# Accumulating row transfers, the gate's first weights behind the last experts, and statistics tied to the neighbouring tile, in a one-core decoder layer

## The chip, the cores and the metric

The kernel runs on one core of a Trainium2 chip. Its engines are TensorE (PE, with PEld for its weight loads), VectorE (DVE), ScalarE (ACT), GpSimd (POOL) and SyncE (SP, which here only issues transfers); 16 DMA engines move data. The metric is the device time of one execution in microseconds, as the median of several runs.

## The reference, cut to what matters

One layer over 512 tokens of 2048 numbers, all float32:

```python
y = concat([s5(u), conv(v, g)]) @ w_o + b_o
h = layer_norm(alpha * x + y, ln1)
m = hierarchical_moe(h)            # 32 experts, 2 per token; hidden width 256
h = layer_norm(alpha * h + m, ln2)
e = (p @ w_p) * sigmoid(h @ w_pg + b_pg)
x = layer_norm(alpha * h + e, ln3)
```

In the mixer every token's two experts compute `silu(t @ w_gate) * (t @ w_up)`, weighted, times `w_down`; `m` is the sum of the two results.

## The kernel before, in words

Tokens are 4 tiles of 128 (`NT`), features 16 chunks of 128 (`KD`). The first part (input projection, state space group, convolution group, output projection, first layer norm, routing) ends at about 675 us and is not touched. `p @ w_p` is made there too and kept in DRAM (`p_dram`), but for the last token tile's, which comes later at line 1210; until then the two `raw` buffers hold `w_p`.

**Experts (lines 1077 to 1282).** The 32 experts are packed in 14 groups (`GROUPS`) of 128 token slots; a group holds 1, 2 or 4 experts. For each group `gather` fetches its 128 token rows from `h_dram` into `gx` (an indirect transfer from POOL's queue), `columns` transposes them into `xt`, `up` multiplies by the gate and up weights in four quarters, `act` makes the activations `at`, `down` multiplies by the down weights in two halves, and `scatter` writes the result rows to `y_dram` (two indirect transfers, one for each half of the columns; two rows for each token, one for each of its experts). All weights come once, in 192 loads of 1 MiB from SP's queue (`ring_load`) into a ring of buffers: 15 of its own at first, and after group 1 the two `raw` buffers, which line 1213 puts at the head of the ring. A load waits until the products on its buffer's former contents are done, and SP issues in order. Loads of the first group and two quarters of the second are called for ahead (`early`, `ahead1`).

In the round of group 0 stands a branch (line 1226) for experts with more tokens than their slots: all engines read a count `mo` and jump over its body where there is none, as with these inputs. The gather and transposes of group 1 follow it. `mo` lies in a column of `xt`.

**Tail (lines 1285 to 1437).** `tt[m]`, called `h2[m]` here, holds alpha times the first layer norm's result. `total(m)` loads the two y rows of each token of tile m (two transfers for each half of the columns), adds them, adds the sum to `h2[m]` and takes the statistics; `normalize(m)` makes the layer norm in four quarters, transposes each and splits it in two parts of reduced precision, `h2h` (ACT) and `h2l` (DVE). The product with `w_pg` goes in four column blocks c; each weight quarter of 1 MiB is split by `wsplit` in two halves of two parts (`whi` by ACT, `wlo` by DVE or POOL), and each product is three matmuls (`mm3`, lines 100 to 102). Block 0 goes tile by tile, right behind `normalize`; `gate` applies bias, sigmoid and `p`; block 3 ends with the last layer norm and the output.

The order on each engine's queue is set at build time by a planner that runs the program against a model of durations; engines then work through their queues in order, and a wait holds what is behind it. Pools release memory at `close()`, and a later tile in the same place waits for the former one's readers.

Of the kernel before, what the change touches and what calls it, by code (L numbers as in the profile page):

```python
# [8 lines left out]
FT = mybir.dt.float32  # L9
# [8 lines left out]
P = 128  # L18
# [36 lines left out]
def build(tc, I, out, dbg=None, stages=9):  # L55
# [1021 lines left out]
    s5 = top.enter_context(ExitStack())  # L1077
    if True:
        psE = s5.enter_context(tc.tile_pool(reuse_waits="tile", name="psE", bufs=1, space=PSUM))
        ep = s5.enter_context(tc.tile_pool(reuse_waits="tile", name="ep", bufs=1))  # L1080
# [4 lines left out]
        def big(name):  # L1085
            return ep.tile([P, D], FT, name=name)
# [11 lines left out]
        gx = big("gx")  # L1098
        ring += [big(f"ring{n}") for n in (13, 14)]
        ring = [ring[0], *ring[4:], last, ring[1], ring[2], ring[3]]  # L1100
        turn = [0]

        def ring_load(src):
            t = ring.pop(0)
            ring.append(t)
            nc.sync.dma_start(t, src)
            return t
# [80 lines left out]
        ahead1 = [loads(1, 0)]  # L1188
        gather(sl1)
        V.tensor_copy(ids_, tab[:, 0:NP])  # L1190
        columns()
        for i, (width, members) in enumerate(GROUPS):
            st = strips(width, members)
            gu = bank("gu", 2)
            if i + 1 < NGR and i:
                gather(sl0[:, i + 1:i + 2])
            for q in range(4):
                up(gu, st, early[q] if i == 0 else ahead1[q] if i == 1 and q < 2 else loads(i, q), q)
            at = act(gu, wt0[:, i:i + 1])
            if i + 1 < NGR and i:  # L1200
                columns()
            for q in range(2):
                down(at, st, early[4 + q] if i == 0 else loads(i, 4 + q), q, sl0[:, NGR + i:NGR + i + 1])
            if i == 1:

                for q in range(2):
                    for c in range(2):
                        ps = bank("dps", 4)
                        for k in range(2):
                            T.matmul(ps, pm[:, k], wps[q][:, k, c * 512:(c + 1) * 512], start=k == 0, stop=k == 1)  # L1210
                        (A.copy if c else V.tensor_copy)(pe_[:, c], ps)
                    G.dma_start(p_dram[NT - 1, 2 * q:2 * q + 2].rearrange("c p d -> p c d"), pe_)
                ring[:0] = [rpool.tile([P, D], FT, name="raw", tag="raw", bufs=2) for _ in range(2)]
            if i == 2:
# [7 lines left out]

            mo = xt[:, 0, 0:1].bitcast(I32)
            V.tensor_copy(mo, tab[:, 2 * NP:])
            most = nc.values_load(mo[0:1], min_val=0, max_val=S)
            with tc.If(most > 0):
# [28 lines left out]
                with tc.For_i(0, NP, 1) as n:  # L1255
                    mine = nc.values_load(tab[0:1, bass.ds(n + NP, 1)], min_val=0, max_val=S)
                    with tc.If(mine > 0):
                        e = bass.ds(nc.values_load(tab[0:1, bass.ds(n, 1)], min_val=0, max_val=NE - 1), 1)
                        for c in range(NOV):
                            with tc.If(mine > c * P):  # L1260
# [17 lines left out]
                                V.memset(gx, 0.0)  # L1278
            gather(sl0[:, 1:2])
            columns()  # L1280

# [3 lines left out]
    with ExitStack() as s5:  # L1285
# [20 lines left out]
        for n in range(2):  # L1306
            V.tensor_copy(pick[n], ident[0:8, 4 * n:4 * n + 4].unsqueeze(2).broadcast_to([8, 4, P]))

        raws = [rpool.tile([P, D], FT, name="raw", tag="raw", bufs=2) for _ in range(2)] + [fy.tile([P, D], FT, name=f"fr{n}") for n in range(2)]
        for q in range(3):  # L1310
            nc.sync.dma_start(raws[q], I["w_pg"][0, q])
        y0 = [fy.tile([P, 2, 1024], FT, name=f"y0{c}") for c in range(2)]
        hls = [wsplit(wF, raws[q], 8, (V, V) if q else (G, G)) for q in range(3)]
        for n in range(8):
# [4 lines left out]

        def load_y(r, m, c):  # L1320
            for q in range(2):
                nc.sync.dma_start(r[:, :, q * 512:(q + 1) * 512], yv[c][m, :, :, q * 512:(q + 1) * 512])

        for c in range(2):
            load_y(y0[c], 0, c)
        nc.sync.dma_start(raws[3], I["w_pg"][0, 3])
        hls.append(wsplit(wF, raws[3], 8, (G, G)))
        w_pg = ahead([lambda c=c, q=q: wsplit(wF, raw_load(I["w_pg"][c, q]), 8) for c in range(1, 4) for q in range(4)], 1)
# [26 lines left out]
        def total(m):  # L1355

            t = h2[m]
            st2 = fh.tile([P, 4, 6], FT, name="st2", bufs=2)
            if m:
                rs = [rpool.tile([P, 2, 1024], FT, name="raw", tag="raw", bufs=2) for _ in range(2)]  # L1360
                for c in range(2):
                    load_y(rs[c], m, c)
            else:
                rs = y0
            for c, r in enumerate(rs):
                for q in range(2):
                    i = slice(q * 512, (q + 1) * 512)
                    o = t[:, c * 1024 + q * 512:c * 1024 + (q + 1) * 512]
                    (G if m or q == 0 else V).tensor_tensor(r[:, 0, i], r[:, 0, i], r[:, 1, i], op=OP.add)
                    (G if m and not (m == 1 and q) else V).tensor_tensor(o, o, r[:, 0, i], op=OP.add)  # L1370
                    V.bn_stats(st2[:, 2 * c + q], o)
            return st2
# [18 lines left out]
        st2 = total(0)  # L1391
        fystk.close()
        fp = s5.enter_context(tc.tile_pool(reuse_waits="tile", name="fp", bufs=1))
        h2h = fp.tile([P, KD, S], FR, name="h2h")
# [108 lines left out]
```

## Time and profile before

| | us |
|---|---|
| Median of 3 runs | 1488.04 (1487.8 to 1489.32) |
| Profiled execution, its own time | 1486.21 |
| Its span, first to last instruction | 1484.5 |
| PE busy | 1264.4 (85%) |
| DVE busy | 784.1 (53%) |
| POOL busy | 392.9 (26%) |
| ACT busy | 376.4 (25%) |

Busy matmuls overlap one another, so a busy TensorE need not be at its peak; shares are means over stages with different limits, so a stage is read from its own window. The chain of waits is followed back from the last instruction to what released each step. A wait for several things is put down to the one that came last. SP's issues are not counted as busy; its waits have a view of their own. Where a line is a helper's (lines 79, 80, 100 to 102, 166 to 181), instructions are told apart by the tiles that they name.

### The profile page before, as it was taken

How to read it: one execution, taken by the hardware profiler on the slowest of the kernel's cores; microseconds unless marked ns; L12 is line 12 of the kernel's file. 1: busy time of each engine (PE TensorE's matmuls, PEld its weight loads, DVE VectorE, ACT ScalarE, POOL GpSimd, SP SyncE). 2: the span in 40 equal slices, each digit the busy share in tenths (PEclk: the TensorE clock that was granted, in tenths of full speed). 3: DMA queues.
4: the chain of work that ended last, by engine and by line, in shares of the span. 5: the costliest groups of instructions: out<-in, count | busy, mean ns of one | idle time of the engine just before them, and what ended most of it. 6: DMA issues, size and time to landing. Idle time of an engine off the chain costs nothing.

```text
span 1484.5 us, 16536 instructions
## 1 busy us (share of the span) xinstructions
PE 1264.4 (85%) x6128; PEld 805.0 (54%) x6129; DVE 784.1 (53%) x1275; ACT 376.4 (25%) x568; POOL 392.9 (26%) x327
## 2 busy tenths in 40 slices
PE   6999999989999999978488998787767774599996
PEld 4877878777777888843132322221111121388884
DVE  7999899789997643681011110010000006975567
ACT  4336555554333421121012100000000003023210
POOL 0368667864944200010010110000000005600000
PEclk9999999998999999989699999999889996699998
DMA  6344544536531362349659999999999995426413
GB/s 233 110 132 119 153 145 137 146 115 217 218 120 59 115 223 85 110 175 375 271 220 424 422 422 421 420 419 420 418 409 418 415 386 190 142 105 215 141 44 120
DMA packets 97448, 349.90 MB, mean 236 GB/s; under 512 B 29939, under 2 KB 43779, under 8 KB 61707
## 3 DMA queue, kind: packets, MB, share of 16 engines
q1 hardware_dynamic: 51152, 303.21, 52.4%
q10 hardware_dynamic: 38832, 21.38, 5.3%
q0 software_dynamic: 7376, 24.19, 4.2%
q8 instruction: 50, 0.82, 0.2%
q14 instruction: 38, 0.30, 0.1%
HBM read 324.36 MB, written 36.38 MB: 243 GB/s over the span
## 4 chain that ended last, share of the span: by engine, by line
DMA 27%; PE 19%; DVE 4%; issue 1%; ACT 0%; POOL 0%; SPq 0%; DVEq 0%; POOLq 0%; ACTq 0%
DMA ring<-w_gu 16%; DMA ring<-w_dn 8%; PE gu L1144 4%; PE fps L102 3%; PE fps L101 3%; PE fps L100 3%; PE dps L1165 2%; DMA raw<-w_gu 2%; DVE tt L180 1%; PE xtp L1124 1%; DMA gx<-h_dram,sl 1%; DVE tt L181 1%; PE h2p L102 0%; PE h2p L101 0%; PE h2p L100 0%
## 5 line engine op out<-in xcount | busy, mean ns | idle before, releaser
L1144 PE MATMUL gu<-ring,xt 128*32 128x512 f32 (+2 forms) x1112 | 241.3, 654 | 57.2 <-DMA ring<-w_gu 57.2
L237 DVE SCALAR_TENSOR_TENSOR cps<-hc,wdw,cps 128x512 f32<-128x512 f32 x232 | 175.0, 754 | 4.8
L1144 PEld LDWEIGHTS gu<-ring,xt 128*32 128x32 f32 (+2 forms) x1112 | 63.4, 130 | 207.1 <-issue 109.4
L100 PE MATMUL zp<-xh,whi 128*128 128x512 f32 x384 | 157.0, 410 | 10.3 <-ACT whi L79 10.1
L79 ACT CAST whi<-raw 128x1024 fp32r<-128x1024 f32 x116 | 119.4, 1047 | 169.3 <-PE zp L102 58.8
L102 PE MATMUL zp<-xh,wlo 128*128 128x512 f32 x384 | 154.2, 402 | 2.7 <-DVE wlo L80 2.7
L101 PE MATMUL zp<-xl,whi 128*128 128x512 f32 x384 | 154.7, 403 | 1.6 <-DVE xl L80 1.6
L80 DVE TENSOR_TENSOR wlo<-raw,whi 128x1024 fp32r<-128x1024 f32 x90 | 125.6, 1405 | 55.2 <-ACT whi L79 54.3
L1151 DVE TENSOR_TENSOR act<-act,gu 128x256 f32<-128x256 f32 x14 | 5.9, 421 | 240.9 <-ACT act L1150 240.9
L1165 PE MATMUL dps<-ring,at 128*32 128x512 f32 (+2 forms) x520 | 121.1, 621 | 10.1 <-ACT at L1156 5.1
L1114 POOL DMA_INDIRECT y_dram<-ob,sl x28 | 27.8, 993 | 340.3 <-ACT ob L1167 340.0
L1129 DVE COPY xt<-xtp 128x512 f32<-128x512 f32 x28 | 19.4, 692 | 143.1 <-PE xtp L1124 135.0
L80 POOL TENSOR_TENSOR wlo<-raw,whi 128x1024 fp32r<-128x1024 f32 x26 | 70.4, 2707 | 85.8 <-ACT whi L79 73.3
L100 PE MATMUL fps<-whi,h2h 128*128 128x512 f32 x224 | 89.5, 400 | 0.7 <-ACT h2h L79 0.7
L102 PE MATMUL fps<-whi,h2l 128*128 128x512 f32 x224 | 89.7, 401 | 0.0
L101 PE MATMUL fps<-wlo,h2h 128*128 128x512 f32 x224 | 88.9, 398 | 0.0
L100 PEld LDWEIGHTS zp<-xh,whi 128*128 128x128 f32 x384 | 73.5, 192 | 26.2 <-ACT whi L79 10.2
L102 PEld LDWEIGHTS zp<-xh,wlo 128*128 128x128 f32 x384 | 73.3, 191 | 20.6 <-DVE wlo L80 3.9
L101 PEld LDWEIGHTS zp<-xl,whi 128*128 128x128 f32 x384 | 73.4, 191 | 17.3 <-DVE xl L80 2.0
L1165 PEld LDWEIGHTS dps<-ring,at 128*32 128x32 f32 (+2 forms) x520 | 35.6, 128 | 80.6 <-issue 57.9
L1167 DVE COPY ob<-dps 128x512 f32<-128x512 f32 x28 | 19.3, 691 | 103.7 <-PE dps L1165 103.7
L1124 PE MATMUL xtp<-ident,gx 128*128 128x128 f32 x224 | 37.2, 290 | 33.2 <-DMA gx<-h_dram,sl 21.0
(460 smaller groups left out, 2273.0 us busy)
## 6 DMA issues: line engine op xcount, KB each, us to landing
ring<-w_gu SPq DMA_DIRECT2D x117, 1024.0 KB, 21.6
ring<-w_dn SPq DMA_DIRECT2D x55, 1024.0 KB, 20.7
raw<-w_in SPq DMA_DIRECT2D x24, 1024.0 KB, 4.9
raw<-w_o SPq DMA_DIRECT2D x16, 1024.0 KB, 4.8
raw<-w_pg SPq DMA_DIRECT2D x14, 1024.0 KB, 5.5
raw<-w_gu SPq DMA_DIRECT2D x11, 1024.0 KB, 21.8
raw<-w_dn SPq DMA_DIRECT2D x9, 1024.0 KB, 22.2
raw<-y_dram SPq DMA_DIRECT2D x12, 512.0 KB, 5.7
```

The source lines that it names most:

```text
L79: A.copy(hi, src)
L80: eng.tensor_tensor(lo, src, hi.bitcast(FT), op=OP.subtract)
L100: T.matmul(ps, lh, rh, start=start, stop=False)
L101: T.matmul(ps, lh, rl, start=False, stop=False)
L102: T.matmul(ps, ll, rh, start=False, stop=stop)
L237: V.scalar_tensor_tensor(ps if k < 30 else acc, hc[:, k:k + S], wdw[:, ct, k:k + 1], ps, op0=OP.mult, op1=OP.add)
L1114: G.indirect_dma_start(out=y_dram[q], out_offset=bass.IndirectOffsetOnAxis(ap=isc, axis=0), in_=ob[:, q * 1024:(q + 1) * 1024], in_offset= ...
L1124: T.transpose(ps[:, kk * P:(kk + 1) * P], gx[:, k * P:(k + 1) * P], ident)
L1129: V.tensor_copy(o, ps)
L1144: T.matmul(gu[cols], xt[:, k, cols], raws[j][:, kk * 512:(kk + 1) * 512], start=k == 0, stop=k == KD - 1)
L1165: T.matmul(outs[c][cols], at[:, k, cols], raws[j][:, o:o + 512], start=k == 0, stop=k == 1)
L1167: (A.copy if c else V.tensor_copy)(ob[:, q * 1024 + c * 512:q * 1024 + (c + 1) * 512], outs[c])
```

## The change

- Two buffers of the ring, `kept`, lie in a pool of their own at the other end of SBUF and outlive the expert stage, in the place of `ring13` and `ring14`. The two `raw` buffers come to the end of the ring and not to its head, and the products of line 1210 come in group 3's round and not in group 1's.
- For the last 17 loads (`count[0] > 6 * NE - NRING`) the four `kept` buffers are skipped. After the last group, DVE writes one column of each from `at`, and then the first four quarters of `w_pg` are loaded into them; their splits are all on DVE.
- Group 1's gather and transposes come in group 0's round, ahead of the branch; the branch's body does them again at its end. `mo` is a tile of its own, made from a column of `xt` times zero plus the count.
- `total(m)` no longer loads y and adds it on POOL and DVE. `add_y(m, j)` adds the j-th row of each token straight to `h2[m]` in SBUF by two accumulating transfers from POOL's queue. Tile 0's second row is a plain load `y1` and an addition on DVE. Tiles 1 to 3 are first touched by a small DVE instruction that reads tile 0 behind its accumulation; their rows are then added in the order written below.
- The statistics of tile m (m > 0) are preceded by a small DVE instruction that reads the last columns of `h2l` of tile m-1.

```diff
+        kstk = top.enter_context(ExitStack())
+        kp = kstk.enter_context(tc.tile_pool(reuse_waits="tile", name="kp", bufs=1, side="right"))
...
-        ring += [big(f"ring{n}") for n in (13, 14)]
-        ring = [ring[0], *ring[4:], last, ring[1], ring[2], ring[3]]
-        turn = [0]
+        kept = [kp.tile([P, D], FT, name=f"kept{n}") for n in range(2)]
+        ring = [ring[0], *ring[4:], *kept, last, ring[1], ring[2], ring[3]]
+        turn, count = [0], [0]
 
         def ring_load(src):
+            count[0] += 1
             t = ring.pop(0)
+
+            while count[0] > 6 * NE - NRING and any(t is k for k in kept):
+                t = ring.pop(0)
             ring.append(t)
             nc.sync.dma_start(t, src)
             return t
...
+        mo = ep.tile([P, 1], I32, name="mo")
         V.tensor_copy(ids_, tab[:, 0:NP])
         columns()
+        V.scalar_tensor_tensor(mo, xt[:, 0, 0:1], 0.0, tab[:, 2 * NP:], op0=OP.mult, op1=OP.add)
...
-            if i + 1 < NGR and i:
+            if i + 1 < NGR:
                 gather(sl0[:, i + 1:i + 2])
...
-            if i + 1 < NGR and i:
+            if i + 1 < NGR:
                 columns()
...
-            if i == 1:
+            if i == 3:
...
-                ring[:0] = [rpool.tile([P, D], FT, name="raw", tag="raw", bufs=2) for _ in range(2)]
+                kept += [rpool.tile([P, D], FT, name="raw", tag="raw", bufs=2) for _ in range(2)]
+                ring += kept[2:]
...
-            mo = xt[:, 0, 0:1].bitcast(I32)
-            V.tensor_copy(mo, tab[:, 2 * NP:])
...
-            gather(sl0[:, 1:2])
-            columns()
+                gather(sl0[:, 1:2])
+                columns()
+
+
+        for q in range(4):
+            V.tensor_copy(kept[q][:, 0:1], at_[NGR % 2][:, 0, 0:1])
+            nc.sync.dma_start(kept[q], I["w_pg"][0, q])
...
-        raws = [rpool.tile([P, D], FT, name="raw", tag="raw", bufs=2) for _ in range(2)] + [fy.tile([P, D], FT, name=f"fr{n}") for n in range(2)]
-        for q in range(3):
-            nc.sync.dma_start(raws[q], I["w_pg"][0, q])
-        y0 = [fy.tile([P, 2, 1024], FT, name=f"y0{c}") for c in range(2)]
-        hls = [wsplit(wF, raws[q], 8, (V, V) if q else (G, G)) for q in range(3)]
+        y1 = fy.tile([P, D], FT, name="y1")
+        hls = [wsplit(wF, kept[q], 8) for q in range(2)]
...
-        def load_y(r, m, c):
-            for q in range(2):
-                nc.sync.dma_start(r[:, :, q * 512:(q + 1) * 512], yv[c][m, :, :, q * 512:(q + 1) * 512])
+        def add_y(m, j):
+
+            for c in range(2):
+                G.dma_start(h2[m][:, c * 1024:(c + 1) * 1024], yv[c][m, :, j], accum_op=OP.add)
 
         for c in range(2):
-            load_y(y0[c], 0, c)
-        nc.sync.dma_start(raws[3], I["w_pg"][0, 3])
-        hls.append(wsplit(wF, raws[3], 8, (G, G)))
+            nc.sync.dma_start(y1[:, c * 1024:(c + 1) * 1024], yv[c][0, :, 1])
+        add_y(0, 0)
+        for m in range(1, NT):
+
+            o = h2[m].rearrange("p (c d) -> p c d", c=2)[:, :, 0]
+            V.scalar_tensor_tensor(o, h2[0][:, 0:2], 0.0, o, op0=OP.mult, op1=OP.add)
+        for m, j in ((1, 0), (2, 0), (1, 1), (3, 0), (2, 1), (3, 1)):
+            add_y(m, j)
+        hls += [wsplit(wF, kept[q], 8) for q in range(2, 4)]
...
             if m:
-                rs = [rpool.tile([P, 2, 1024], FT, name="raw", tag="raw", bufs=2) for _ in range(2)]
-                for c in range(2):
-                    load_y(rs[c], m, c)
-            else:
-                rs = y0
-            for c, r in enumerate(rs):
-                for q in range(2):
-                    i = slice(q * 512, (q + 1) * 512)
-                    o = t[:, c * 1024 + q * 512:c * 1024 + (q + 1) * 512]
-                    (G if m or q == 0 else V).tensor_tensor(r[:, 0, i], r[:, 0, i], r[:, 1, i], op=OP.add)
-                    (G if m and not (m == 1 and q) else V).tensor_tensor(o, o, r[:, 0, i], op=OP.add)
-                    V.bn_stats(st2[:, 2 * c + q], o)
+
+                o = t.rearrange("p (q d) -> p q d", q=4)[:, :, 0]
+                V.scalar_tensor_tensor(o, h2l[:, KD - 1, m * P - 4:m * P].bitcast(FT), 0.0, o, op0=OP.mult, op1=OP.add)
+            for q in range(4):
+                o = t[:, q * 512:(q + 1) * 512]
+                if m == 0:
+                    V.tensor_tensor(o, o, y1[:, q * 512:(q + 1) * 512], op=OP.add)
+                V.bn_stats(st2[:, q], o)
             return st2
...
         st2 = total(0)
         fystk.close()
+        kstk.close()
```

## Rows read from the trace of the kernel before

**Rows 1.** The page's 40 slices of 37.1 us: GB/s moved in each
```profile
GB/s 233 110 132 119 153 145 137 146 115 217 218 120 59 115 223 85 110 175 375 271 220 424 422 422 421 420 419 420 418 409 418 415 386 190 142 105 215 141 44 120
```

**Rows 2.** Chain that ended last, by time: start us, us, engine or transfer, line
```profile
714.43 9.47 DMA gx<-h_dram,sl
744.79 0.39 ACT act L1150
756.93 7.08 PE dps L1210 x16
1220.04 3.66 PE gu L1144 x14
1235.87 2.09 DMA y_dram<-ob,sl
```

**Rows 3.** Waits of SP's queue, 685 to 765 us: total us, times, longest
```profile
SPq L1106 <- PE dps L1210: 32.6, 2, 29.8
SPq L1226 <- SPq L1226: 22.4, 2, 17.1
```

**Rows 4.** SP's timeline, 700 to 765 us: start us, us, instructions
```profile
705.74 1.82 SPq L1106 DMA_DIRECT2D ring<-w_dn  x4
760.59 3.77 SPq L1106 DMA_DIRECT2D raw<-w_gu  x2
```

**Rows 5.** The branch's line L1226, 720 to 735 us: duration ns, first and last start
```profile
L1226 SPq EVENT_SEMAPHORE  x8: 17/17/17, 730.0 to 730.6; - x8
```

**Rows 6.** Windows: length, busy us of PE, PEld, DVE, ACT, POOL, PEclk, DMA, GB/s
```profile
730.60:760.60 30.00, 28.53 (x125) 10.65 (x122) 4.87 (x8) 3.59 (x8) 4.06 (x4) 0.98 0.20 70
764.60:1220.00 455.40, 355.51 (x1780) 110.66 (x1780) 41.28 (x71) 41.70 (x71) 32.87 (x33) 0.95 1.01 418
1267.60:1284.00 16.40, 15.51 (x60) 12.02 (x60) 15.07 (x26) 1.76 (x3) 8.62 (x7) 0.79 0.41 137
1284.00:1300.00 16.00, 3.25 (x13) 2.36 (x14) 15.89 (x18) 1.17 (x2) 14.54 (x10) 0.63 0.55 188
1300.00:1340.00 40.00, 40.00 (x186) 32.95 (x185) 28.14 (x64) 11.96 (x16) 0.00 (x0) 0.94 0.36 122
1340.00:1469.50 129.50, 129.50 (x573) 107.04 (x571) 82.90 (x128) 27.84 (x33) 0.00 (x0) 1.00 0.36 126
```

**Rows 7.** TensorE's timeline, 1264 to 1268 us
```profile
1265.77 1.09 PE L1385 MATMUL h2p<-ident,tt 128*128 128x128 f32 x4 [21.41 <-DVE mean L1352]
1267.57 0.80 PE L100 MATMUL fps<-whi,h2h 128*128 128x512 f32 x1 [0.72 <-ACT h2h L79]
```

**Rows 8.** TensorE's timeline, 655 to 760 us: group 0's down products
```profile
694.26 8.79 PE L1165 MATMUL dps<-ring,at 128*64 128x512 f32 x32 [0.46 <-ACT at L1156]
```

**Rows 9.** Waits of SP's queue, 1100 to 1215 us
```profile
SPq L1106 <- DMA ring<-w_gu: 48.5, 23, 3.0
SPq L1106 <- PE gu L1144: 2.2, 7, 0.4
```

**Rows 10.** ScalarE's timeline, 1222 to 1230 us
```profile
1225.66 0.37 ACT L1156 COPY at<-atp 128x256 f32<-128x256 f32 x1 [1.56 <-PE atp L1155]
```

**Rows 11.** VectorE's groups, 1301 to 1340 us: count, busy us, mean ns
```profile
L80 DVE TENSOR_TENSOR wlo<-raw,whi 128x1024 fp32r<-128x1024 f32 x4 | 4.9, 1223 | 0.8 <-ACT whi L79 0.7
L180 DVE SCALAR_TENSOR_TENSOR tt<-tt,mean,g 128x512 f32<-128x512 f32 x6 | 4.1, 747 | 0.0
L166 DVE SCALAR_TENSOR_TENSOR lnq<-lny,lnu 128x1 f32<-128x1 f32 x6 | 1.3, 218 | 0.2
```

**Rows 12.** Transfers by line: count, KB each, median us from issue to landing
```profile
p_dram<-eh POOLq DMA_DIRECT2D x3, 512.0 KB, 3.2
y<-y_dram SPq DMA_DIRECT2D x4, 512.0 KB, 6.9
```

**Rows 13.** VectorE's groups, 1255 to 1299 us
```profile
L180 DVE SCALAR_TENSOR_TENSOR tt<-tt,mean,g 128x512 f32<-128x512 f32 x6 | 6.7, 1175 | 0.0
L1371 DVE BATCH_NORM_STATS2 st<-tt 128x6 f32<-128x512 f32 x9 | 6.0, 684 | 1.2 <-POOL tt L1370 1.1
```

## The prediction

> **What bounds the kernel now.** I read the 40 slices first: from 779 us on, the DMA engines move about 420 GB/s for eleven slices, and between one slice of 375 and these stand two of 271 and 220 GB/s [rows 1]. So the expert weights are a stream that sets its own pace, and it has a hole near its start. The chain of waits says the same from the other end: the last gate and up weights land at 1220.0, and whatever shortens the stream moves everything behind it [rows 2]. The hole is read from the waits of SP, the engine that issues the loads: between 685 and 765 it waited 29.8 us at a stretch for the products of L1210, the embedding of the last token tile [rows 3]. SP's own timeline gives its place: last load of group 1 issued at 707.6, first load of group 2 at 760.59, into a `raw` buffer [rows 4], because line 1213 puts the two `raw` buffers, which still hold `w_p`, at the head of the ring. Ahead of this wait stands another, at the branch of L1226: SP leaves it at 730.6 [rows 5]. In 730.6 to 760.6 DMA ran at 70 GB/s; in 764.6 to 1220 at 418 [rows 6].
>
> The second place is the tail. The final gate's first product runs at 1267.57 [rows 7], then 16.4 us in which TensorE is nearly full, 16.0 us in which it works 3.25, and from 1300 to 1469.5 no gap at all [rows 6]. So the tail is set by when tile 0 starts and by the hole ahead of tile 1; behind the last product, at 1469.5, come 15.0 us to the span's end that the change leaves alone.
>
> **The change part by part.**
>
> *Ring order, L1210 at group 3, group 1's tokens ahead of the branch.* The wait on L1210 goes. What is late next is the branch (730.6), which stays. The ring now has 15 slots; load 24, the first of group 2, takes the slot of load 9 (15 back), whose products ended by 703 [rows 8]; 25 and 26 follow in the slots of 10 and 11. Group 1's own products must free the rest. Today TensorE stands still from the branch until the gather of group 1, issued at 714.43, has landed 9.47 us later [rows 2]; with that gather issued in group 0's place and its transposes ahead of the branch, group 1 starts some 6 us behind group 0's end (four transposes, the branch; an estimate), at 709. From 723.9 it needed 20.9 us to its activation at 744.79 [rows 2], so from 709 it has freed eight more slots by 730. So SP issues at 730.6 what it now issues at 760.6: 30.0 us. Not all is gained: the 30.0 us at 70 GB/s moved 2.1 MB of gathers, scatters and `p`, which will now lie in the stream and cost 2.1 MB / 418 GB/s = 5 us. **Gain 25 us**; bounds 0 (another wait holds the queue) and 30. The 7.1 us of L1210 [rows 2] move into a stretch where TensorE works 355 of 455 us [rows 6]: nothing, since the stream covers it; without that cover 7. On POOL's queue the gather is moved past group 0's two scatters, which wait for products that end at 703; it delays neither.
>
> *Four buffers withheld from the last 17 loads.* SP's waits late in the stream are 48.5 us on earlier loads landing against 2.2 us on gate and up products [rows 9]: it is paced by loads in flight, not by slots, so 13 slots instead of 17 cost nothing. If slots bound, at most four loads of 2.5 us (1.05 MB at 418 GB/s), 10 us.
>
> *First gate weights behind the last activations.* Four loads of 1 MiB start when `at` is there (1226.03 [rows 10]) and DVE has written four single columns; 4.2 MB at 418 GB/s end near 1238. The wait for y covers them until about 1246; if DVE's copies come behind the last `ob` copies they end 8 us later, about when they are needed. Four half splits move from POOL to DVE, 4 x 1.22 = 4.9 us [rows 11], in the same wait. I count 0, bounds 0 and 8.
>
> *y by accumulating transfers.* Fourteen transfers of 512 KB from POOL's queue, in seven pairs, and two plain ones replace sixteen loads of 512 KB, 24 POOL additions and some on DVE. The trace has no accumulating transfer. Nearest from below: a pair moves 1.05 MB, 2.5 us at 418 GB/s; from above: two `y<-y_dram` loads one after the other, 2 x 6.9 = 13.8 us [rows 12]. The old tile must be read as well as the row, so I take twice the lower one, 5 us, plus the 2.1 us that the last scatter needed to land [rows 2]. The other POOL row, 3.2 us for a plain 512 KB [rows 12], is nearer to this than to 13.8.
>
> The Trainium skill (Collectives: The Full Stack, "The bandwidth ceiling: the fold count and why AG ≠ RS ≠ AR") says that an add on the DMA path costs two source reads where a copy costs one, which halves the rate; no run here shows it yet. By that page's rule a pair would cost 5 us and the sum would stand; by the plain rate it would be 2.5 us and tile 0 would start 2.5 us sooner.
>
> Tile 0: scatter landed at 1238.0; two issues 1.5; 2.1 + 5 for the pair: 1246.6. A split still running on DVE: 1. Four additions and four statistics, 8 x 0.69 = 5.5 [rows 13]; the small steps of the root, a dozen at 0.15 to 0.22 [rows 11], 2.5; scale and shift of the first quarter 2 x 0.75; transposes, cast and first issue 1.8 [rows 7]. Sum 1258.9. First product at about **1259** instead of 1267.6: 8.6 us. DVE runs these at the free price, since POOL adds nothing meanwhile: today the scale beside POOL's additions takes 1.18 us [rows 13] against 0.75 once they are over [rows 11].
>
> Tiles 1 to 3: the 16.0 us hole goes, because the statistics of tile 1 no longer wait on POOL nor the root on its port. In its place comes the tie: statistics of tile m queue on DVE behind the last `h2l` of tile m-1. From there it is 2.8 (statistics) + 2.5 + 1.5 + 1.0 = 7.8 us to the first product of tile m, while TensorE has about two quarters of tile m-1 left, 24 products of 129.5 us / 576 = 0.225 [rows 6], 5.4 us. I count 2.2 us of stall three times, 6.6. (The two quarters are an estimate; with three there would be no stall.) Behind the tie on DVE's queue stand only splits of column 1's weights. The ties of tiles 1 to 3 to tile 0's pair wait on DVE too; the splits of the last two quarters, 4.9 us, can queue behind them, but tile 0's first two quarters of products do not need these: 0, bounds 0 and 5. The adds must be in time: with 5 us a pair, the third pair behind tile 0's (tile 1's second) lands at 1264, the fifth at 1274, the sixth at 1279, against needs of about 1270, 1285 and 1300: up to 7 us a pair they hide. **Gain 8.6 + 16.0 - 6.6 = 18 us**; bounds: 28 (no tie stall, plain price) and, at 13.8 us a pair, a loss: the seventh pair lands at 1241 + 97 = 1338, and 7.8 + 13.3 (a third of the 40 us of rows 6) later TensorE is done with column 0 at 1359 instead of 1340, 19 us lost.
>
> **Sum.** Span 1484.5 - 25 - 18 = 1441.5. The profiled execution took 1486.21, 1.7 us around its span, and lies 1.8 us below the median of 1488.04. So the median expected is 1441.5 + 3.5 = **1445**, 2.9% faster.
>
> **Rivals.**
> A. *Accumulating transfers at twice my price* (10 us a pair). First product 1264, tile 1's last pair at about 1282, later tiles paced by pairs; column 0 ends at 1337, tail gain 3. Span 1456.5, median **1460**. For it: loads of y take 6.9 us each today; against: these share the engines with two other transfers.
> B. *The stream starts no earlier.* The branch at 730.6 is followed by a wait of the same length on something else, a slot not yet free or a later join. Tail alone: 1466.5, median **1470**. For it: the branch already costs SP 22.4 us in two waits [rows 3]; against: the slots of loads 9 to 11 had their last reader at 703.
> C. *Slower: additions serialized in the transfer path*, say 20 us a pair. Seven pairs end at 1381, column 0 at 1402, 62 us lost against 25 gained: span 1521.5, median **1525**. It turns slower from 14.6 us a pair, above which the last tile starts more than 25 us late. For it: two transfers into one tile must land one before the other, and none was ever timed here; against: transfers into three tiles can overlap.
> D. *The change cancels itself*: B together with a dearer tail, within 0.2%.
>
> **How the numbers follow.** Forecast 53%, with its own range 1430 to 1456; A 17%, B 14%, C 13%, D 3%. About 0.2%, 3 us, is what measurement here can tell from no change. Faster: forecast, A and B, 0.84; same 0.03; slower 0.13. The range runs from 1430 (both gains near their upper bounds) past A and B to 1478; left out are C, D and a little below.
>
> **What would show it.** Right: SP's first load of group 2 follows the branch at once and into a ring slot; DMA near 418 GB/s from about 733; last weights landed near 1195; no POOL additions; first gate product about 39 us behind the landing, with short gaps ahead of tiles 1 to 3. Wrong: SP still idle after its branch (B); a pair that takes 10 us or more from issue to landing and DVE waiting for it (A, C); DMA gaps in the last 17 loads (withheld slots).

## The result, and the profile after

The median of three runs is 1454.62 us (1453.62 to 1456.86) against 1488.04: a ratio of 0.9776, 95% interval 0.9754 to 0.9798. That is 33.4 us gained where the forecast had 43, 1454.6 against 1445. The profiled execution's span is 1452.8 us against 1484.5, 31.7 less, and the last landing of weights divides it (all in us; the column "forecast" has the gain that was forecast):

| | before | after | gained | forecast |
|---|---|---|---|---|
| last gate and up weights landed | 1220.04 | 1193.18 | 26.9 | 25 |
| from the landing to the first gate product | 47.5 | 47.6 | 0 | 8.6 |
| from the first to the last gate product | 201.9 | 197.1 | 4.8 | 16.0 - 6.6 = 9.4 |
| from the last product to the end | 15.0 | 14.9 | 0.1 | 0 |

So the front did what was forecast, and the tail gave 4.8 us of its 18. The question of the experiments is where those 13 us are. (Less 1.9 us that the front gave beyond its 25, and 1.7 by which the medians moved more than the spans, they are the 10 us between 43 and 33.4.)

**The front.** The 40 slices of 36.3 us, GB/s moved, answer to [rows 1]: in the two slices ahead of the steady 420, where 271 and 220 stood, there are now 406 and 369.

```profile
GB/s 228 123 132 116 134 123 155 173 111 135 302 116 96 88 228 88 0 304 271 406 369 424 422 422 418 419 417 418 416 408 413 417 322 238 172 99 201 149 43 117
```

The waits of SP's queue, 685 to 765 us (total us, times, longest), against [rows 3]: the 29.8 us for the embedding products are gone, the branch stays, and only waits of up to 4.5 us on loads and down products follow it.

```profile
SPq L1233 <- SPq L1233: 24.0, 2, 18.6
SPq L1112 <- DMA ring<-w_gu: 14.8, 6, 4.5
SPq L1112 <- PE dps L1171: 7.3, 4, 3.7
```

SP's timeline (start us, us, instructions), against [rows 4]: the first load of group 2 is issued at 729.67 and not at 760.59, right at the branch's end.

```profile
702.99 1.82 SPq L1112 DMA_DIRECT2D ring<-w_dn  x4
729.67 0.97 SPq L1112 DMA_DIRECT2D kept<-w_gu  x2
```

Windows of the stream's start (columns as in [rows 6], the number of instructions in brackets): 219 GB/s for the 3.4 us in which the stream fills, then 419, where 730.6 to 760.6 had 70.

```profile
729.60:733.00 3.40, 3.40 (x17) 1.07 (x14) 0.00 (x0) 0.00 (x0) 0.00 (x0) 1.00 0.68 219
733.00:760.00 27.00, 24.59 (x84) 10.21 (x84) 4.39 (x8) 3.48 (x7) 3.02 (x3) 1.00 1.01 419
```

**The tail.** The chain of waits (start us, us, step), against [rows 2]: three accumulating transfers stand in it, the first pair (8.85), then of tile 1's two rows the first (7.50) and the second (20.20 from issue to landing).

```profile
1193.18 3.66 PE gu L1150 x14
...
1213.08 8.85 DMA tt<-y_dram
...
1222.95 7.50 DMA tt<-y_dram
...
1230.73 20.20 DMA tt<-y_dram
```

POOL's issues behind the ties, 1220 to 1230 us: six in a row, then one behind a landing. A second row into a tile waits for the first, so the six are the first rows of tiles 1 to 3.

```profile
1222.41 5.19 POOL L1331 DMA_DIRECT2D tt<-y_dram  x6 [7.44 <-DVE tt L1339]
1228.41 0.84 POOL L1331 DMA_DIRECT2D tt<-y_dram  x1 [0.82 <-DMA tt<-y_dram]
```

VectorE's timeline, 1209 to 1252 us (in brackets: idle us before it, and what ended that). Ties are the small instructions that make a tile wait: those of line 1339 hold tiles 1 to 3 for tile 0's pair, that of line 1377 a tile's statistics for the tile before. The ties of line 1339 wait 11.01 us for the first pair; behind them, between its landing and the aggregate at 1235.03, stand seven half splits of weights (`wlo`). Tile 1's tie, line 1377, waits 1.00 for the second row.

```profile
1209.71 1.23 DVE L80 TENSOR_TENSOR wlo<-kept,whi 128x1024 fp32r<-128x1024 f32 x1 [0.86 <-ACT whi L79]
1221.95 0.31 DVE L1339 SCALAR_TENSOR_TENSOR tt<-tt,tt 128x2 f32<-128x2 f32 x3 [11.01 <-DMA tt<-y_dram]
1222.17 2.35 DVE L80 TENSOR_TENSOR wlo<-kept,whi 128x1024 fp32r<-128x1024 f32 x2
1224.44 1.29 DVE L1381 TENSOR_TENSOR tt<-tt,y 128x512 f32<-128x512 f32 x2
1225.64 1.22 DVE L80 TENSOR_TENSOR wlo<-kept,whi 128x1024 fp32r<-128x1024 f32 x1
1226.78 1.22 DVE L80 TENSOR_TENSOR wlo<-raw,whi 128x1024 fp32r<-128x1024 f32 x1
...
1228.52 1.21 DVE L80 TENSOR_TENSOR wlo<-raw,whi 128x1024 fp32r<-128x1024 f32 x1
...
1231.44 2.36 DVE L80 TENSOR_TENSOR wlo<-raw,whi 128x1024 fp32r<-128x1024 f32 x2
...
1235.03 0.27 DVE L176 BATCH_NORM_AGGREGATE lnmv<-st 128x2 f32<-128x24 f32 x1
...
1251.06 0.17 DVE L1377 SCALAR_TENSOR_TENSOR tt<-h2l,tt 128x4 f32<-128x4 f32 x1 [1.00 <-DMA tt<-y_dram]
```

TensorE's first gate product, against [rows 7]:

```profile
1240.76 0.80 PE L100 MATMUL fps<-whi,h2h 128*128 128x512 f32 x1 [0.80 <-ACT h2h L79]
```

From the first to the last gate product, before and after: TensorE's busy time and what is left of the window, its idle time, which was 13.6 us and is 6.1. The number of its instructions is the same; its busy time is 2.8 us more.

```profile
1267.57:1469.50 201.93, 188.29 (x828) 154.40 (x828) 142.03 (x233) 42.73 (x54) 23.16 (x16) 0.94 0.38 131
```

```profile
1240.76:1437.90 197.14, 191.07 (x828) 155.07 (x828) 130.94 (x234) 42.44 (x54) 1.70 (x2) 0.96 0.39 125
```

Windows ahead of tiles 1 and 2 and behind. The 16 us hole of [rows 6] has become gaps: TensorE works 1.80 of 4 us ahead of tile 1, and then its granted clock, 1.00 before, is 0.59 of full speed in the next 4 us; at 1276 it falls again, to 0.72.

```profile
1256.00:1260.00 4.00, 1.80 (x8) 0.74 (x7) 3.83 (x10) 0.58 (x1) 0.00 (x0) 1.00 1.07 212
1260.00:1264.00 4.00, 3.55 (x11) 2.94 (x12) 2.83 (x5) 0.58 (x1) 0.00 (x0) 0.59 0.06 11
1272.00:1276.00 4.00, 3.19 (x16) 2.10 (x14) 3.75 (x11) 0.58 (x1) 0.00 (x0) 1.00 0.00 0
1276.00:1280.00 4.00, 3.15 (x12) 2.35 (x11) 3.48 (x6) 0.59 (x1) 0.00 (x0) 0.72 0.00 0
```

### The profile page after: what moved, and what is told of

Same layout as the page of the kernel before. It is cut to its first block, busy times and chain, and to the rows that moved or that the text cites. A ratio compares the mean times of both kernels' runs of the same rounds, so it can differ in the third digit from the quotient of the medians.

```text
span 1452.8 us, 16515 instructions
## 1 busy us (share of the span) xinstructions
PE 1271.5 (88%) x6128; PEld 808.3 (56%) x6129; DVE 762.3 (52%) x1285; ACT 377.0 (26%) x568; POOL 361.4 (25%) x313
## 4 chain that ended last, share of the span: by engine, by line
PE 39%; DMA 29%; DVE 20%; issue 4%; POOL 3%; ACT 2%; ACTq 1%; SPq 1%; DVEq 0%; POOLq 0%
DMA ring<-w_gu 10%; DMA ring<-w_dn 7%; DVE cps L237 6%; PE gu L1150 6%; PE zp L100 4%; PE zp L101 4%; PE zp L102 4%; DMA raw<-w_gu 3%; PE dps L1171 3%; DMA kept<-w_gu 3%; PE fps L102 3%; PE fps L100 3%; PE fps L101 3%; DMA tt<-y_dram 3%; DVE wlo L80 2%
## 5 line engine op out<-in xcount | busy, mean ns | idle before, releaser
L1150 PE MATMUL gu<-ring,xt 128*32 128x512 f32 (+2 forms) x992 | 235.5, 670 | 45.7 <-DMA ring<-w_gu 45.5
L80 DVE TENSOR_TENSOR wlo<-raw,whi 128x1024 fp32r<-128x1024 f32 x92 | 119.8, 1310 | 52.4 <-ACT whi L79 51.6
L1171 PE MATMUL dps<-ring,at 128*32 128x512 f32 (+2 forms) x464 | 124.8, 613 | 11.0 <-DMA ring<-w_dn 5.9
L100 PEld LDWEIGHTS zp<-xh,whi 128*128 128x128 f32 x384 | 73.9, 193 | 26.9 <-ACT whi L79 10.3
L80 POOL TENSOR_TENSOR wlo<-raw,whi 128x1024 fp32r<-128x1024 f32 x24 | 65.6, 2734 | 85.2 <-ACT whi L79 72.6
L1156 ACT ACTIVATE act<-gu 128x256 f32<-128x256 f32 x14 | 5.4, 383 | 199.0 <-PE gu L1150 199.0
```

Source lines behind the costliest of these rows:

```text
L80: eng.tensor_tensor(lo, src, hi.bitcast(FT), op=OP.subtract)
L100: T.matmul(ps, lh, rh, start=start, stop=False)
L1150: T.matmul(gu[cols], xt[:, k, cols], raws[j][:, kk * 512:(kk + 1) * 512], start=k == 0, stop=k == KD - 1)
L1171: T.matmul(outs[c][cols], at[:, k, cols], raws[j][:, o:o + 512], start=k == 0, stop=k == 1)
```

## The experiments

Three causes offered themselves. **T1**: the ties on DVE hold the splits back until the first pair lands, and these then stand in tile 0's way. **T2**: the accumulating transfers pace tile 1, so that an earlier tile 0 gains nothing. **T3**: the tie of the statistics to the last low part opens the gaps, and the clock falls behind them. Each kernel below ran five times (the plain rows four, the tail alone twelve) beside the kernel before; a ratio is to that, with its 95% interval. A single execution has its own luck of a few us, in the first part (up to 670 us), in the clock and, up to 3 us, between the last landing and the first gate product. So traces are compared by times behind the last landing and by the steps between, and times by ratios.

**The front alone** (`front_only`): the first half of the diff, without `kept` outliving the stage, with the tail of before.

> The front part of the change alone: the two raw buffers at the end of the ring, the last tile's embedding products in group 3's round, group 1's gather and transposes ahead of the branch; no withheld buffers, and the tail of the kernel before (plain loads of y, additions on POOL). Theory 1 (the stream's gain of 26.9 us, read from the last landing at 1193.2 against 1220.0, goes through to the end whole, and the tail adds only what is left): 26 to 27 us faster, about 1461. Rival (the two parts lean on one another: without the tail's part some of the stream's gain is lost again before the end): 20 us faster or less, 1468 or more.

Measured: 1462.36 against 1486.36, 0.9823 (0.98 to 0.9847). Last landing at 1197.38, 263.2 us before the end (before: 264.5). By the ratio that is 26 us, as expected: the front's gain goes through whole.

**The tail alone**: the other half, with the old ring order, line 1210 in group 1's round and the gather behind the branch.

> The tail part alone: accumulating transfers, withheld buffers, the first gate weights behind the last activations, the ties; the front as in the kernel before. From the traces (264.5 us behind the last landing before, 259.6 after): 5 us faster, about 1483. Rival (the tail's part is worth the 18 us forecast, and the whole change loses some of it only because its stream ends in another state): 15 us or more faster, 1473 or less.

Measured: 1481.91 against 1486.36, 0.9966 (0.9948 to 0.9985). By the ratio the tail is worth 5 us, as expected. The two halves add up: 1.77% and 0.34% make 2.11%, against 2.24% (2.02 to 2.46) for the whole.

**The ring order alone**, on the kernel before:

```diff
-            if i == 1:
+            if i == 3:
...
-                ring[:0] = [rpool.tile(...) for _ in range(2)]
+                ring += [rpool.tile(...) for _ in range(2)]
```

> The kernel before with the ring order alone: the two raw buffers at the end of the ring and the last tile's embedding products in group 3's round; group 1's gather and transposes stay behind the branch, the tail is as before. Theory (the wait for the embedding products was the hole; three slots are free at the branch, and group 1's products, from 724 on, free the rest about as fast as loads fill them): 19 to 23 us faster, 1465 to 1469. Rival (without the early gather, group 1's products are late and SP waits for their slots as long as it waited for the embedding): 10 us or less, 1476 or more.

Measured: 1462.67 against 1488.14, 0.9844 (0.9821 to 0.9867), the same as the whole front within the noise. By the ratio that is 23 us, the upper end of what was expected. Its SP, 685 to 765 us and at the branch's end:

```profile
SPq L1226 <- SPq L1226: 19.3, 2, 14.2
SPq L1106 <- PE gu L1144: 15.8, 6, 3.5
```

```profile
731.15 3.01 SPq L1106 DMA_DIRECT2D ring<-w_gu  x4
```

Without the early gather SP waits 15.8 us in short pieces for group 1's products; with it (the front alone) it waits 12.5 us for earlier loads to land instead. From SP's first load behind the branch to the last landing it is 465.8 us without the early gather (731.15 to 1196.99) and 463.3 to 463.7 in the ten traces with it. The prediction thought the early gather necessary to free the slots; by the traces it is worth some 2 us, which the times can't tell from nothing.

**Ties on POOL** (T1 against T2): the ties of line 1339 as two steps on POOL.

```diff
+        tz = fh.tile([P, 2], FT, name="tz")
+        G.tensor_scalar(tz, h2[0][:, 0:2], 0.0, None, op0=OP.mult)
...
-            V.scalar_tensor_tensor(o, h2[0][:, 0:2], 0.0, o, op0=OP.mult, op1=OP.add)
+            G.tensor_tensor(o, o, tz, op=OP.add)
```

> The changed kernel, with the three ties of tiles 1 to 3 to tile 0's accumulation written on POOL instead of DVE, so that no split of the gate's weights queues behind them. Theory T1 (tile 0's start is late because seven half splits stand behind the waiting ties on DVE): tile 0's statistics end 6 us sooner, at about 1229, and the span is 5 to 6.5 us shorter, about 1448.5. Rival T2 (tile 1's second row lands at 1250.9 whatever DVE does, so tile 0 may start sooner, but TensorE then waits that much longer ahead of tile 1): first gate product at about 1235 but the span less than 1.5 us shorter, 1453 to 1455, with a gap of 7 to 8 us ahead of tile 1.

Measured: 1453.23, 0.9775 (0.9757 to 0.9794): no gain that shows. The first product came 43.2 us behind the last landing (1194.02) instead of 47.6. Of these 4.4 us the ties have 2.5: from DVE's first step behind the pair (the ties or an addition) to the aggregate it takes 13.1 us in all six traces with the ties on DVE, and 10.6 in the three with the ties on POOL and the splits as they were. The rest is the execution's: in a second trace of the changed kernel (below) the first product comes 44.6 us behind the landing. TensorE then stood still ahead of tile 1, while tile 1's tie on DVE waited for its second row:

```profile
1237.26 0.80 PE L100 MATMUL fps<-whi,h2h 128*128 128x512 f32 x1 [0.80 <-ACT h2h L79]
1258.86 1.08 PE L1398 MATMUL h2p<-ident,tt 128*128 128x128 f32 x4 [6.53 <-DVE mean L1369]
```

```profile
1220.93 1.29 DVE L1383 TENSOR_TENSOR tt<-tt,y 128x512 f32<-128x512 f32 x2 [8.23 <-POOL tz L1337]
...
1231.52 0.26 DVE L176 BATCH_NORM_AGGREGATE lnmv<-st 128x2 f32<-128x24 f32 x1
...
1252.20 0.17 DVE L1379 SCALAR_TENSOR_TENSOR tt<-h2l,tt 128x4 f32<-128x4 f32 x1 [6.26 <-DMA tt<-y_dram]
```

So T1 delays tile 0's start, and T2 takes back what is gained there. Five half splits stayed among tile 0's additions and statistics in DVE's order, so T1 was taken away only in part.

**Row order** (T2), with the ties on POOL: tile 3 tied to tile 1's second row, so that its transfers can't come ahead of that row.

```diff
-        for m, j in ((1, 0), (2, 0), (1, 1), (3, 0), (2, 1), (3, 1)):
-            add_y(m, j)
...
+        for m, j in ((1, 0), (2, 0), (1, 1), (2, 1)):
+            add_y(m, j)
+        G.tensor_scalar(tz[1], cols(1), 0.0, None, op0=OP.mult)
+        G.tensor_tensor(cols(3), cols(3), tz[1], op=OP.add)
+        for j in range(2):
+            add_y(3, j)
```

> The changed kernel with the ties on POOL (as in the run before on that) and the rows in another order: first rows of tiles 1 and 2, second rows of tiles 1 and 2, and tile 3 tied to tile 1's second row, so that tile 3's transfers can't share the engines with tile 1's. Theory T2 (after the ties moved, tile 1 waits for its second row, which shares the engines with tile 3's first): that row lands at about 1240 instead of 1252, the gap ahead of tile 1 shrinks from 6.5 to 2.3 us, and the span is 4 us shorter than with the ties on POOL alone, 1447 to 1449. Rival (the accumulating transfers fill the engines in any order, or the in-order queue on POOL loses between two rows what the order gains): the row lands after 1247 and the span is 1451 or more.

Measured: 1447.02, 0.973 (0.9711 to 0.9749), the time that T2 gave. Tile 1's tie now comes 54.7 us behind the last landing (1189.41) instead of 58.2, after a wait of 0.20. The row itself did not come as early as T2 had it: 54.4 us behind the landing, where the 1240 of the expectation would have been 46 and the rival's 1247 would have been 53. So the order brings the row forward by less than thought. TensorE's idle time between the first and the last gate product is 5.3 us against 10.8 with the ties on POOL alone. VectorE's ties of tiles 1 to 3:

```profile
1244.06 0.17 DVE L1385 SCALAR_TENSOR_TENSOR tt<-h2l,tt 128x4 f32<-128x4 f32 x1 [0.20 <-POOL tz L1346]
...
1259.24 0.17 DVE L1385 SCALAR_TENSOR_TENSOR tt<-h2l,tt 128x4 f32<-128x4 f32 x1
...
1274.51 0.17 DVE L1385 SCALAR_TENSOR_TENSOR tt<-h2l,tt 128x4 f32<-128x4 f32 x1
```

**Statistics tied to the third quarter** (T3): `KD - 1` in line 1377 becomes 11, in the changed kernel and then in the row order's.

> The changed kernel, with the statistics of tile m tied to the third quarter (chunk 11) of tile m-1's low part and not to the last (chunk 15). Theory T3 (the tie leaves TensorE without work for about 2.3 us ahead of each of tiles 1 to 3, and each gap is followed by 2 to 4 us at half the granted clock, 1.5 us more): the gaps ahead of tiles 2 and 3 go, 7 to 8 us, and the first as well if tile 1's row has landed by then, 11 in all: 1443 to 1447. Rival T2 (the accumulating transfers pace tiles 1 to 3): the gaps stay where they are, 1453 to 1455. Rival (DVE's order only moves the wait: the last quarter of tile m-1 is now late behind the statistics and the root of tile m, and TensorE stands within the tile): 1452 to 1458 with gaps inside the tiles.

> The kernel before this one in the list (ties on POOL, tile 1's rows ahead of tile 3's), with the statistics of tile m tied to the third quarter of tile m-1's low part as well. If T1, T2 and T3 hold together: tile 0 starts 3.5 us sooner, no gap ahead of tiles 1 to 3 and no fall of the granted clock behind it, 3 x 3.8 us: 14 to 15 us less than the changed kernel, 1438 to 1441. Rival (only the tie to the last quarter counts): as the run with that tie alone, 1446 to 1448.

Measured: 1447.58, 0.975 (0.973 to 0.977), and 1446.73, 0.9723 (0.9703 to 0.9743). The first lies half a microsecond above T3's range, but its interval overlaps the changed kernel's; the second was to give 1438 to 1441 and gives what the row order gives alone, as its rival had it. A tile does become shorter: tie to tie it is 13.7 and 13.9 us in the second kernel, 15.2 and 15.3 in the row order. But tile 1's tie, due sooner, waits 4.43 us for its row, and TensorE stands 3.7 us around that tile's start; in all it is idle for 5.2 us between the first and the last gate product, where the row order has 5.3:

```profile
1249.43 0.17 DVE L1385 SCALAR_TENSOR_TENSOR tt<-h2l,tt 128x4 f32<-128x4 f32 x1 [4.43 <-POOL tz L1346]
...
1263.17 0.17 DVE L1385 SCALAR_TENSOR_TENSOR tt<-h2l,tt 128x4 f32<-128x4 f32 x1
...
1277.08 0.17 DVE L1385 SCALAR_TENSOR_TENSOR tt<-h2l,tt 128x4 f32<-128x4 f32 x1
```

**Plain rows**: `accum_op=OP.add` taken out of `add_y`; the kernel leaves the additions out, the rows overwrite `h2`.

> The changed kernel with plain transfers in place of the accumulating ones; the additions are left out, so h2 is overwritten by the rows. It is there for the price of a transfer. If the addition halves the rate of the engines (210 GB/s in the changed kernel while nothing but these transfers ran, 418 for plain loads): a pair takes 2.5 us less, the first pair lands about 6.4 us after its issue instead of 8.85, the seven pairs are through by about 1240 instead of 1259, and the time is 2.5 (tile 0) + 1 (tile 1's wait) us shorter, about 1451. Rival (the transfers are paced by POOL's issues and by the wait for the row before, not by the rate): 1453 to 1455 and the seven pairs not through before 1252.

Measured: 1444.88, 0.9713 (0.9689 to 0.9736), more than either side expected. Why it is more than the 3.5 us expected is not shown. In its trace the span ends 250.9 us behind the last landing, against 259.6 in the changed kernel's first trace and 254.6 in its second (below); TensorE is busy for 188.2 us between the first and the last gate product, as in the second (188.0) and not as in the first (191.1), so part of the difference to the first is the clock. POOL's first issue and DVE's ties show the first pair through in 5.2 us instead of 8.85 (7.6 in the second trace):

```profile
1211.84 0.58 POOL L1331 DMA_DIRECT2D tt<-y_dram  x1 [3.46 <-DMA y_dram<-ob,sl]
```

```profile
1217.02 0.30 DVE L1339 SCALAR_TENSOR_TENSOR tt<-tt,tt 128x2 f32<-128x2 f32 x3 [7.69 <-DMA tt<-y_dram]
```

and a window with the engines full has the price: 425 GB/s here, where only plain transfers move (rows and two loads of `w_pg`), against 211 in the changed kernel, where only accumulating rows move.

```profile
1232.00:1236.00 4.00, 1.24 (x5) 0.87 (x5) 3.72 (x11) 0.59 (x1) 0.00 (x0) 0.50 1.03 425
```

```profile
1252.00:1256.00 4.00, 4.00 (x19) 3.34 (x18) 3.79 (x13) 0.00 (x0) 0.00 (x0) 1.00 1.07 211
```

A pair of 1.05 MB is 5.0 us at 211 GB/s and 2.5 at 425. The Trainium skill's rule that the prediction weighed (Collectives: The Full Stack, "The bandwidth ceiling: the fold count and why AG ≠ RS ≠ AR") is stated there for the reduce-scatter of the collectives: its add reads two sources, and its rate is about half of a copy's. The rate in these traces agrees, at 0.50; that the second read is the reason, no run here shows.

**The changed kernel again, and with spare products** (T3's clock). The second kernel puts ten products that nobody reads behind tiles 0 to 2, eight of them in the gap.

```diff
+                if c == 0 and m < NT - 1:
+                    if m == 0:
+                        spare = bank("fps", 6)
+                    for _ in range(10):
+                        T.matmul(spare[:, 0:512], h2h[:, KD - 1, m * P:(m + 1) * P], hls[3][1][0][:, 1024 - 512:], start=True, stop=True)
```

> The changed kernel once more, on the chip of the two runs that follow, so that they have it beside them, and for a second trace of it. If the fall of the granted clock behind the three gaps ahead of tiles 1 to 3 belongs to this kernel, the new trace shows it three times again, 4 us in all; if it came by chance, it shows none to two. Time: 1453 to 1457.

> The changed kernel with ten more products for each of tiles 0 to 2, whose result nobody reads: eight stand right behind the tile's last product on TensorE's queue, that is in the gap ahead of the next tile, two among the products ahead of it. 2.25 us of work at full clock, two thirds to all of the gap. If the falls of the clock behind the gaps cost what the trace of the changed kernel suggests (4 us), and an engine that works on keeps its clock: 2 to 4 us less than the changed kernel beside it. Rival (the falls cost nothing on the path, or have another cause than the gap): the same within 1 us, or up to 2 us more, since 0.45 us a tile stand ahead of needed products.

Measured: 1452.81, 0.9757 (0.9735 to 0.9779), and 1454.88, 0.9769 (0.9746 to 0.9792): the same. The traced execution of the unchanged program was its fastest, 1444.64, and its clock fell behind one gap and not behind the other two. Its first product, its ties, 16.8 us apart where the clock fell and 15.2 where it did not, and its windows at the gaps ahead of tiles 1 and 2:

```profile
1232.91 0.80 PE L100 MATMUL fps<-whi,h2h 128*128 128x512 f32 x1 [0.80 <-ACT h2h L79]
```

```profile
1244.13 0.17 DVE L1377 SCALAR_TENSOR_TENSOR tt<-h2l,tt 128x4 f32<-128x4 f32 x1 [3.10 <-DMA tt<-y_dram]
...
1260.90 0.17 DVE L1377 SCALAR_TENSOR_TENSOR tt<-h2l,tt 128x4 f32<-128x4 f32 x1
...
1276.13 0.17 DVE L1377 SCALAR_TENSOR_TENSOR tt<-h2l,tt 128x4 f32<-128x4 f32 x1
```

```profile
1250.00:1254.00 4.00, 2.69 (x9) 1.73 (x10) 3.96 (x8) 0.58 (x1) 0.00 (x0) 0.55 0.75 147
...
1268.00:1272.00 4.00, 2.47 (x12) 1.72 (x12) 4.00 (x8) 1.17 (x2) 0.00 (x0) 1.00 0.00 0
```

So a fall costs 1.5 us a tile, and three falls do not belong to the kernel: how many there are differs between its executions. With the spare products the clock fell once in three as well, so these two traces do not show that filling a gap holds the clock; with the products' own work the ties are 17.7 and 16.45 us apart, with and without a fall.

**Late splits** (T1 all but one half split, with T2): ties on POOL, rows in strict order, and the splits of quarters three and four held by a column that reads tile 0's first low part.

```diff
...
+                    if m == 0:
+                        for q in range(2, 4):
+                            V.scalar_tensor_tensor(kept[q][:, 0:1], h2l[:, 3, 0:1].bitcast(FT), 0.0, kept[q][:, 0:1], op0=OP.mult, op1=OP.add)
+                            hls.append(wsplit(wF, kept[q], 8))
```

> The changed kernel with the first cause taken away wholly: the ties are on POOL, and the splits of the third and fourth weight quarter are tied to the first low part of tile 0, so that none of these four half splits (4.9 us) stands on DVE between the landing of tile 0's pair and its first product; the rows come in strict order (tile 1's first, then tile 1's second with tile 2's first, then tile 2's second with tile 3's two). T1 and T2 together: tile 0's first product 40 to 41 us behind the last landing instead of 45.5 with the row order alone, tile 1's second row lands before it is needed, and the time is 4 to 5 us below the row order's 1447: 1442 to 1443. Rival (the splits come due as products of tile 0 need them, and only move the wait into the tile): a gap of 3 to 5 us ahead of the third quarter's products, and 1446 or more.

Measured: 1446.84, 0.9719 (0.9698 to 0.974). The time was to be 1442 to 1443 and is the row order's. The first product comes 41.7 us behind the last landing (expected: 40 to 41, the row order had 45.5), and from the pair's landing to the aggregate it is 7.3 us instead of 13.1. The span ends 250.3 us behind the landing, where the row order had 251.9: of the 3.8 us gained at the start 1.6 are left. The rival's gap ahead of the third quarter's products is not there; the next tile's row is late instead, and TensorE's idle time between the first and the last gate product is 7.5 us instead of 5.3:

```profile
1190.39 3.65 PE L1150 MATMUL gu<-ring,xt 128*64 128x512 f32 x14 [1.29 <-DMA ring<-w_gu]
...
1232.04 0.80 PE L100 MATMUL fps<-whi,h2h 128*128 128x512 f32 x1 [0.80 <-ACT h2h L79]
```

```profile
1219.05 0.69 DVE L1391 TENSOR_TENSOR tt<-tt,y 128x512 f32<-128x512 f32 x1 [8.63 <-DMA tt<-y_dram]
...
1226.31 0.26 DVE L176 BATCH_NORM_AGGREGATE lnmv<-st 128x2 f32<-128x24 f32 x1
...
1258.67 0.17 DVE L1387 SCALAR_TENSOR_TENSOR tt<-h2l,tt 128x4 f32<-128x4 f32 x1 [1.47 <-DMA tt<-y_dram]
```

Against the changed kernel on the same chip (0.9757 there, 0.9719 here) it is 0.4% faster, but the intervals overlap a little (0.9735 to 0.9779 and 0.9698 to 0.974). The row order, with or without the tie to the third quarter, and the late splits all lie at 1447, below the changed kernel's 1453 to 1455; which of them is best can't be told.

## Why the prediction was right, and where 10 us are missing

The median lies in the stated range, 1.4 us below its upper end. The mechanism of the front was right. The tail's sum was 13 us too good, and that the time still lies in the range is in part luck, since the front and the medians gave 3.6 us more than forecast.

- **Ring order: right, by its mechanism and nearly its size.** 31 us sooner at the branch, 26.9 at the last landing (25 forecast). The early gather was thought necessary and is worth some 2 us: with it group 1's first product came at 716.62 and not at 709, and without it the loads still went out behind the branch.
- **Withheld buffers, 0: right.** From SP's first load behind the branch to the last landing it is 463.51 us with the withholding (729.67 to 1193.18) and 463.55 without (the front alone, 733.83 to 1197.38).
- **A pair, 5 us and 2.1 of latency: right.** 8.85 us with its issues in the first trace and 7.6 in the second, where 8.6 stood, and 5.0 at the rate of the window.
- **"The splits of the last two quarters, 4.9 us, can queue behind them, but tile 0's first two quarters of products do not need these: 0, bounds 0 and 5": this step failed first.** From the pair's landing to the aggregate it took 13.1 us (1221.95 to 1235.03) and not 6.5. With the splits out of the way it took 7.3 (late splits, 1219.05 to 1226.31), so they cost 5.8. And it was all but one of the eight, not four: those that had time before the landing stood behind the ties too, in DVE's order. In the first trace the pair was also issued 19.9 us behind the last landing and not 18.0; these 1.9 us, the 6.6 by which 13.1 exceeds 6.5, and 0.2 of the pair are the missing 8.6. In the second trace the pair was issued at 18.2 and took 1.0 less than forecast; there the late aggregate is all that is left of the delay.
- **"The third pair behind tile 0's (tile 1's second) lands at 1264": this step failed behind it.** That was 26 us behind the first pair's issue; it took 37.9 (1213.08 to 1250.95). POOL issues six transfers, the first rows of tiles 1 to 3, ahead of tile 1's second row, where the prediction took the order of the source, and two loads of `w_pg` share the engines meanwhile. In the changed kernel the late tile 0 hid all but 1.00 us of it. Hence moving the ties alone brought nothing, and with the row put forward as well it was 6 us.
- **"16.0 - 6.6": the mechanism held, two sizes did not.** The stalls are 2.65, 1.66 and 1.67 us ahead of and in the first products of tiles 1 to 3, 6.0 in all, 6.6 forecast (by the prediction's own terms, 7.8 - 5.4, it would have been 2.4 each and not 2.2). But the hole of 16.0 was counted as if TensorE had stood still in all of it, though it worked 3.25 us there [rows 6]: its idle time between the first and the last gate product fell by 7.6, from 13.6 to 6.1, and not by 9.4. And the 828 instructions recorded in that stretch, as many as before, took 2.8 us more, 191.1 and not 188.3: behind all three stalls the clock fell, 1.5 us each, more than was lost to low clocks in this stretch before (0.63 and 0.94 in [rows 6]). 7.6 - 2.8 are the 4.8 us of the table. In the second trace of the same program, with one fall, the instructions took 188.0, so this part is not a property of the change.
- **Rivals.** A (10 us a pair) forecast 1460, nearer in time than 1445, but not by its mechanism: a pair is 5 us. B, C and D did not happen.

What stays open is what decides whether the clock falls behind a gap: in the changed kernel it fell three times in one execution and once in another, behind gaps of 1.66 to 2.65 us in the first; in the row order's trace it stayed at 1.00 behind gaps of 1.7 and 1.8 us.

## What to carry to other kernels

A wait added to one engine has to be priced by all that its queue holds behind it, needed or not: here three ties of 0.3 us together held 8.5 us of weight splits until they stood in the critical chain, which cost 5.8. When one cause of a late start is taken away, ask what lands next: moving the ties alone brought nothing, since the next tile's row was late behind it. For transfers, read the order on the issuing engine's queue, since the order in the source need not be it.

## What the runs showed of the hardware

- An accumulating transfer from DRAM into SBUF moves half of what a plain one moves on the same engines: 211 against 425 GB/s, both with the engines fully busy (the windows of the plain rows and of the changed kernel above).
- In these kernels a second row into a tile is issued only when the first has landed, and POOL's queue waits for that: in the changed kernel's trace it idles up to 4.45 us between two issues. The Trainium skill (DMA: Bandwidth & Descriptors, "Rules for kernel authors") says why it must: an accumulate reads its destination and writes it later, and another write that lands between is lost. No run here shows such a loss.
- Executions of one program differ by up to 10 us (1444.64 to 1454.47 in five of the changed kernel). Of the 9.9 us between its two traced spans, 4.9 lie ahead of the last landing, 3.0 from there to the first gate product and 1.8 from there to the last. Part of it is how often TensorE's granted clock falls to 0.5, the lower level of 1.2 GHz, after it stood still for a moment: the down products of the last group took 8.83 us in the first trace, where their stretch had 0.81, and 7.48 with the ties on POOL, where it was 1.00.
